# One norm chain per retention head, three output units taken together, and weight sums with fewer copies on the load queue

## The chip, the cores and the metric

The kernel runs on one core of a Trainium2 chip. A core has TensorE (PE in the profile: matmuls, with its weight loads in a row of their own, PEld), VectorE (DVE), ScalarE (ACT), GpSimd (POOL), a sync engine (SP) that only issues transfers, and 16 DMA engines shared by all queues. The metric is the time of one execution in device microseconds, the median of several runs. Each engine works through its own instructions in a fixed order, so an instruction that waits holds up all that stands behind it on that engine.

## What is computed

One decoder layer on 2048 tokens of 1024 channels: a mixer (retention heads beside a pooling mixer), a cross-attention into 256 memory tokens, and a gated MLP. The change lies in the mixer and in the preparation of weights:

```python
h = rmsnorm(x, mix_norm_g[l])
proj = h @ w_in[l]
q, k, v, g, u = jnp.split(proj, [R, 2 * R, 3 * R, 4 * R], axis=-1)
y_ret = jax.nn.silu(g) * head_rmsnorm(retention(q, k, v, positions), ret_gn_g[l])
y_pool = pool_mixer(u, pool_w[l], pool_scale[l])
x = x + jnp.concatenate([y_ret, y_pool], axis=-1) @ w_out[l]
x = x + cross_attn(rmsnorm(x, xa_norm_g[l]), mem_n, xa_wq[l], xa_wkv[l], xa_wo[l])
x = x + conv_glu_ffn(rmsnorm(x, ffn_norm_g[l]), ffn_w_up[l], ffn_conv_w[l], ffn_conv_b[l], ffn_w_down[l])
```

Retention has four heads of 128 channels and works in chunks of 128 tokens with a state carried from chunk to chunk. Each head's output is normalized per token (`head_rmsnorm`), gated by `silu(g)`, and goes with the four pooled groups into the output projection `w_out`.

## The kernel before, in words

**Blocks.** The 2048 tokens are two blocks of T = 1024, each of two halves of SUB = 512. A block goes through the mixer, the output projection and the attention; the MLP of both blocks follows at the end. Every product in full precision is three matmuls (high times high, high times low, low times high: `passes`, lines 265 to 269), so every tile that is a matmul operand is first split by ACT and DVE into a high and a low part (`split`, line 256, ACT at line 259, DVE in the helper at line 242).

**Order.** The text of the program gives priorities. A planner that simulates the engines then writes each engine's order from it, ahead of the run. `tc.issue_after(ins)` adds one rule: what is written inside the block is put behind `ins` on the engine of `ins`. Generators are stepped along the main loop: `behind[0]` holds the retention of a head, `under[0]` holds `weight_sums` (line 939).

**Mixer of the second block** (`head_projections`, line 1514). Eight "members" of two column groups each (`PAIRS`) are computed with seven items instead of eight; an item is 12 matmuls. The members are, in order, the pool groups 3 and 2 with a gate, the heads, and last the pool groups 0 and 1. When a member has given the second of q and k of a head, the head's `retention` (line 745) is stepped behind the seven items of the next member; the last head, 3, runs behind the last member. After each item two `step()` calls go on with the pooling windows (`pool_steps`), and in the last items `settle()` (line 1644) splits finished tiles into the places that the operand tables have left. The eight results are the tiles 0 to 3 (heads) and 4 to 7 (pool groups) of `mix`.

**Retention of a head** handles two halves a and c of four chunks. Each half has `scores` (PE line 766, transposes of k at 768), `states` (PE 777, then a chain of DVE steps through the four chunks), `values` (PE 790 and 792, then ACT squares at 796, the norm chain on DVE: scale, a reciprocal square root by three Newton steps (`rsqrt`, line 291), scale; then ACT scales at 804) and `mixed` (PE transposes at 809, a DVE step at 812). The steps of the two halves are offset, so that the chain of half a is done while half c is still at its scores. The PSUM tiles of these steps come from `aux()` (line 232), which goes in turn through three banks; the matmuls have five banks (`mmps`).

**Output projection** (`unit`, line 313, called at line 1872). A unit gives 128 output channels of the block: 8 tiles times 2 halves times 3 passes, 48 matmuls in two banks. Its weights are two loads on SP (lines 1869 and 1870) into one raw place, split into two pairs, and its tokens of x (`fetch_x`, line 546) come from two more loads. In the second block unit 0 takes the tiles in the order 7, 6, 0, 1, 2, 5, 3, 4 and all others in the order 0 to 7.

**Weight sums** (`weight_sums`, line 939). The seven-item products need sums of quarters of the weights. 42 jobs make them in DRAM: SP copies four quarters (lines 948 to 950, behind the load last noted in `fetched[0]`), then four accumulating DMAs on POOL's queue add up (lines 952, 953, 956, 959), each waiting for the one before. A job is five steps of the generator. The steps are taken along the main loop, in the attention `pace` of them per table (line 920), with `pace` 1 in the first block and 2 in the second.

Of the kernel before, what the change touches and what calls it, by code (L numbers as in the profile page):

```python
# [136 lines left out]
def trunk(ctx, tc, xT, memT, pos, w_qkgu, w_v, wkv, wqT, wo, wout_r, wout_p, poolT, w_up, w_dn, vecs, consts, outT):  # L137
# [19 lines left out]
    def new_s(dtype):  # L157
        return cp.tile([P, 2 * T], dtype, tag="S", name=nm("S"))

# [9 lines left out]
    S = new_s(F32)  # L169
    raws = Places([(R, j * T) for j in range(3)] + [(S, j * T) for j in range(2)], T)  # L170
# [73 lines left out]
    def ts(eng, out, a, s1, op0, s2=None, op1=None):  # L244
        if op1 is None:
            eng.tensor_scalar(out=out, in0=a, scalar1=s1, scalar2=None, op0=op0)
        else:
            eng.tensor_scalar(out=out, in0=a, scalar1=s1, scalar2=s2, op0=op0, op1=op1)
# [57 lines left out]
    turned = []  # L306
# [6 lines left out]
    def unit(raw, rhs, evac, order=range(KT)):  # L313


        hs = raw if isinstance(raw, list) else pairs(raw)
        ps = [mmps() for _ in range(NS)]
        for h in range(2):
            for s in range(NS):
                for j, k in enumerate(order[4 * h : 4 * h + 4]):  # L320
                    w = [hs[k // 4][:, i, k % 4 * P : (k % 4 + 1) * P] for i in range(2)]
                    passes(ps[s], w, rhs(k, s), h + j == 0, h == 1 and j == 3)
                next(behind[0], None)
                quarter[0] += 1
                if not slow[0] or quarter[0] % 2:
                    next(under[0], None)
                if h == 1:
                    evac(s, ps[s])
# [217 lines left out]
    def fetch_x(b, k):  # L546

        out = []
        for s in range(NS):
            out.append(TT.take())  # L550
            sp.dma_start(out[s].f[:, :SUB], xT[k * P : (k + 1) * P, b * T + s * SUB : b * T + (s + 1) * SUB])
        return out
# [192 lines left out]
    def retention(b, h, qkg, v, out):  # L745
# [4 lines left out]
        def col(ap, c):  # L750
            return ap[:, c * P : (c + 1) * P]
# [4 lines left out]
        class Half:  # L756
# [17 lines left out]
            def states(self):  # L774
                self.kv = aux()
                for c in range(4):
                    pe.matmul(col(self.kv, c), col(self.kn.f, c), self.ch(v, c, h * T), start=True, stop=True)  # L777
                self.cur = [None if b == 0 and self.s == 0 else st]
                for c in range(3):
                    nxt = col(self.kn.f, c)  # L780
                    if self.cur[c] is None:
                        dve.tensor_copy(nxt, col(self.kv, c))
                    else:
                        stt(nxt, self.cur[c], decay[h], col(self.kv, c))
                    self.cur.append(nxt)

            def values(self):
                y = aux()
                for c in range(4):
                    pe.matmul(col(y, c), col(self.pr.f, c), self.ch(v, c, h * T), start=True, stop=self.cur[c] is None)  # L790
                    if self.cur[c] is not None:
                        pe.matmul(col(y, c), self.ch(q, c), self.cur[c], start=False, stop=True)
                stt(st, self.cur[3], decay[h], col(self.kv, 3))
                ss, rr = small(), small()
                for c in range(4):
                    act.activation(col(self.pr.f, c), col(y, c), AF.Square, accum_out=ss[:, c : c + 1])
# [3 lines left out]
                if out is not None:  # L800
                    tt(dve, four(self.kn.f[:, :SUB]), four(y), bcast(rr, P), ALU.mult)
                else:
                    for c in range(4):
                        act.activation(col(self.kn.f, c), col(y, c), AF.Identity, scale=rr[:, c : c + 1])

            def mixed(self):
                mt = aux()
                for c in range(4):
                    pe.transpose(col(mt, c), col(self.kn.f, c), ident)
# [5 lines left out]
                for r in (self.pr, self.kn, gs[self.s]):  # L815
                    r.free()

        a, c = Half(0), Half(1)
        a.scores()
# [14 lines left out]
        if out is not None:  # L834
            q.free()
# [20 lines left out]
    def attention(sums, beside, pace):  # L856
# [39 lines left out]
        for i in range(2 * KT):  # L896
# [23 lines left out]
            for _ in range(pace):  # L920
                next(under[0], None)
# [17 lines left out]
    def weight_sums():  # L939
# [5 lines left out]
        for w, k0, n, to, in jobs:  # L945
            a11, a12, a21, a22 = (block(w, i // 2, i % 2, k0, n) for i in range(4))
            d = [to[i][:, : n * P] for i in range(4)]
            with tc.issue_after(fetched[0].ins):
                for i, a in ((2, a21), (0, a11), (1, a11), (3, a12)):
                    sp.dma_start(d[i], a)  # L950
# [8 lines left out]
            pool.dma_start(d[3], d[1], accum_op=ALU.add, max_dma_last_dim=2048)  # L959
# [554 lines left out]
    def head_projections(b, v, rb, tabs, t1, t2, z3, z4):  # L1514
# [4 lines left out]
        more = new_s(F32R)  # L1519
        raws = Places([(R, j * SUB) for j in range(5)], SUB)  # L1520
        side = Arena(R, 5 * SUB, 1, SUB).take().f
        prs = Places([(Q, j * T) for j in range(3)] + [(more, j * T) for j in range(2)], T)
# [175 lines left out]
        for at, (m, i) in enumerate(items):  # L1698
# [12 lines left out]
            step()  # L1711
            step()
            next(under[0], None)
            if m is members[-1]:
                if i in (1, 2, 4):
                    (t1, t2, t3)[(1, 2, 4).index(i)].free()
                if at >= len(items) - 6:
                    settle()
                    settle()
# [11 lines left out]
        spare = new_s(F32)  # L1731
        raws = Places([(R, j * T) for j in range(3)] + [(spare, j * T) for j in range(2)], T)
        prs = Places([(Q, j * T) for j in range(3)], T)
        return mix, spare
# [87 lines left out]
    for b in range(NB):  # L1822
# [19 lines left out]
        else:  # L1842
# [17 lines left out]
            mix, S = head_projections(b, v, rb, tabs, t1, t2, z3, z4)  # L1860
# [6 lines left out]
        for n in range(KT):  # L1867
# [4 lines left out]
            unit(raw, lambda k, s: [r[:, s * SUB : (s + 1) * SUB] for r in mix[k][1]], add_residual(b, n, xs, got=got), (0, 2, 3, 1, 4, 6, 7, 5) if b == 0 else (7, 6, 0, 1, 2, 5, 3, 4) if n == 0 else range(KT))  # L1872
# [24 lines left out]
        def opening(room, wv):  # L1897
# [3 lines left out]
            for kp in range(KT // 2):  # L1901
                wv.append(value_weights(kp))
# [63 lines left out]
    raws = Places([(R, j * SUB) for j in range(6)] + [(S, j * SUB) for j in range(4)], SUB)  # L1966
# [114 lines left out]
```

## Time and profile before

| | |
|---|---|
| median of 3 runs | 2480.15 us (2478.92 to 2484.32) |
| the profiled execution | 2478.89 us, its span 2477.0 us |
| PE busy | 2422.2 us, 98% of the span |
| DVE busy | 1730.7 us, 70% |
| ACT busy | 1283.2 us, 52% |
| POOL busy | 206.9 us, 8% |
| DMA moved | 501.56 MB, mean 202 GB/s |

The profile is of one execution. Its times are from the start of the span. A view by stretches gives, for each stretch of time, the busy time of each engine, the mean clock granted to TensorE (1.00 is full), the share of the 16 DMA engines that was busy (it can read a little over 1) and what they moved. A line of the view by time reads: start, duration, engine, line of the kernel, operation, output and inputs with their shapes, a count if several were merged, and in brackets the engine's idle time before it with what ended it. The wait view gives in total, times and longest. The stages of the part in question: first block's output projection from about 395 to 480 us, its attention to 575, the attention's output projection to 668, the second block's values to 714, its members to 904, its output projection to 1012, its attention to 1113.

### The profile page before, as it was taken

Reading aid. Unit: us, or ns where it says so; the run is one execution under the profiler, and the core shown is the slowest. Engines: PE = TensorE matmul, PEld = TensorE weight load, DVE = VectorE, ACT = ScalarE, POOL = GpSimd, SP = SyncE. Lnnn points to the kernel's source line nnn. Section 1 sums busy time; section 2 is a strip of 40 time slices with the busy share of each in tenths; the row PEclk is TensorE's granted clock in tenths of the full one; section 3 lists DMA queues with packets and bytes.
Section 4 is the critical chain, followed back from the end, with each engine's and each line's share of the span. In section 5 each row is a group of like instructions: output and inputs, shape, how many; then the busy total and the mean of one; then the engine's idle time right before and its main releaser. Section 6 shows DMA issues by size and latency. Waiting matters only on the chain.

```text
span 2477.0 us, 33287 instructions
## 1 busy us (share of the span) xinstructions
PE 2422.2 (98%) x11294; PEld 2018.0 (81%) x11294; DVE 1730.7 (70%) x2969; ACT 1283.2 (52%) x2303; POOL 206.9 (8%) x272
## 2 busy tenths in 40 slices
PE   6999999999999999999999999999999999999997
PEld 6888888878788877888888888888888888888886
DVE  8645576564676675575678876897667688867876
ACT  6333423443444443434655565665555677666663
POOL 1010111101001131200000010020000000000000
PEclk9999999999999999999999999999999999999998
DMA  8363789727748898966468665665546468768951
GB/s 315 95 167 115 222 209 244 226 51 223 219 125 199 203 258 246 250 204 249 145 198 278 210 190 158 218 222 169 161 154 216 136 223 302 246 189 280 344 171 69
DMA packets 274459, 501.56 MB, mean 202 GB/s; under 512 B 28784, under 2 KB 58096, under 8 KB 274288
## 3 DMA queue, kind: packets, MB, share of 16 engines
q1 hardware_dynamic: 225584, 428.11, 52.4%
q0 software_dynamic: 24192, 43.00, 10.8%
q10 hardware_dynamic: 24512, 28.32, 3.3%
q8 instruction: 89, 1.46, 0.2%
q14 instruction: 82, 0.67, 0.1%
HBM read 398.13 MB, written 187.17 MB: 236 GB/s over the span
## 4 chain that ended last, share of the span: by engine, by line
PE 88%; DMA 5%; DVE 4%; ACT 1%; issue 1%; SPq 0%; POOLq 0%; POOL 0%; ACTq 0%; DVEq 0%
PE mm L267 28%; PE mm L269 28%; PE mm L268 27%; DMA T<-xT 1%; DVE T L242 1%; DMA T<-Xd 1%; DVE Z L242 1%; PE aux L342 1%; PE aux L268 1%; PE aux L267 1%; PE aux L269 1%; PE aux L777 0%; DVE Q L242 0%; DMA T<-pos 0%; DMA Hd<-T 0%
## 5 line engine op out<-in xcount | busy, mean ns | idle before, releaser
L267 PE MATMUL mm<-G,Q 128*128 128x512 f32 (+1 forms) x1720 | 663.2, 386 | 23.5 <-ACT Q L259 14.6
L269 PE MATMUL mm<-G,Q 128*128 128x512 f32 (+1 forms) x1720 | 660.8, 385 | 6.3 <-DVE Q L242 6.1
L268 PE MATMUL mm<-G,Q 128*128 128x512 f32 (+1 forms) x1592 | 609.8, 383 | 0.2 <-DVE G L242 0.2
L268 PE MATMUL mm<-G,E 128*128 128x512 f32 x1084 | 421.6, 389 | 0.0
L267 PE MATMUL mm<-G,E 128*128 128x512 f32 x1084 | 420.2, 390 | 0.0
L269 PE MATMUL mm<-G,E 128*128 128x512 f32 x1084 | 419.2, 389 | 0.0
L267 PEld LDWEIGHTS mm<-G,Q 128*128 128x128 f32 x1720 | 326.6, 190 | 88.9 <-ACT Q L259 15.9
L269 PEld LDWEIGHTS mm<-G,Q 128*128 128x128 f32 x1720 | 326.4, 190 | 70.7 <-DVE Q L242 8.4
L268 PEld LDWEIGHTS mm<-G,Q 128*128 128x128 f32 x1592 | 302.1, 190 | 57.3 <-DVE G L242 1.5
L242 DVE TENSOR_TENSOR Z<-Z,mm 128x512 f32<-128x512 f32 x296 | 201.4, 681 | 101.2 <-PE mm L269 101.0
L251 DVE SCALAR_TENSOR_TENSOR Z<-Z,vecs 128x1024 f32<-128x1024 f32 x176 | 224.5, 1279 | 50.0 <-ACT Z L1104 46.4
L267 PEld LDWEIGHTS mm<-G,E 128*128 128x128 f32 x1084 | 203.5, 188 | 42.4 <-ACT Z L1186 0.3
L269 PEld LDWEIGHTS mm<-G,E 128*128 128x128 f32 x1084 | 203.5, 188 | 42.3
L268 PEld LDWEIGHTS mm<-G,E 128*128 128x128 f32 x1084 | 203.5, 188 | 42.1
L1041 ACT ACTIVATE E<-R 128x512 fp32r<-128x512 f32 (+1 forms) x165 | 101.5, 615 | 142.8 <-PE mm L268 135.3
L242 DVE TENSOR_TENSOR T<-T 128x512 f32<-128x512 f32 (+3 forms) x224 | 152.9, 688 | 23.2 <-ACT T L382 11.1
L242 DVE TENSOR_TENSOR Q<-R,Q 128x512 fp32r<-128x512 f32 x153 | 106.1, 696 | 74.5 <-ACT Q L259 50.8
L242 DVE TENSOR_TENSOR G<-T,G 128x512 fp32r<-128x512 f32 (+1 forms) x181 | 119.0, 673 | 42.5 <-ACT G L990 30.5
L1041 ACT ACTIVATE Q<-R 128x512 fp32r<-128x512 f32 (+1 forms) x157 | 96.9, 618 | 99.6 <-PE mm L268 73.8
L1104 ACT ACTIVATE Z<-Z,vecs 128x1024 f32<-128x1024 f32 x88 | 109.2, 1242 | 35.5 <-DVE Z L242 34.5
L990 ACT ACTIVATE G<-T 128x512 fp32r<-128x512 f32 x157 | 95.9, 625 | 54.5 <-DMA T<-Hd 27.3
L242 DVE TENSOR_TENSOR E<-R,E 128x512 fp32r<-128x512 f32 (+1 forms) x131 | 87.4, 671 | 51.2 <-ACT E L1041 42.3
(308 smaller groups left out, 3666.6 us busy)
## 6 DMA issues: line engine op xcount, KB each, us to landing
T<-Gd SPq DMA_DIRECT2D x168, 256.0 KB, 4.3
Gd<-Z SPq DMA_DIRECT2D x110, 256.0 KB, 2.7
R<-Ud SPq DMA_DIRECT2D x106, 256.0 KB, 2.7
Ud<-w_up SPq DMA_DIRECT2D x88, 256.0 KB, 6.1
R<-w_up SPq DMA_DIRECT2D x80, 256.0 KB, 3.0
S<-Ud SPq DMA_DIRECT2D x70, 256.0 KB, 2.8
T<-xT SPq DMA_DIRECT2D x64, 256.0 KB, 4.2
Gd<-T SPq DMA_DIRECT2D x56, 256.0 KB, 3.3
```

The costliest lines, as they stand in the source:

```text
L242: return eng.tensor_tensor(out=out, in0=a, in1=b, op=op)
L251: dve.scalar_tensor_tensor(out=out, in0=a, scalar=s, in1=b, op0=op0, op1=op1)
L267: pe.matmul(ps, lh, rh, start=start, stop=False, skip_group_check=more)
L268: pe.matmul(ps, lh, rl, start=False, stop=False, skip_group_check=more)
L269: latest[0] = pe.matmul(ps, ll, rh, start=False, stop=stop, skip_group_check=more)
L342: pe.matmul(ps[:, t : t + 1], ap, one, start=True, stop=more is None)
L990: act.activation(hi, x, AF.Copy)
L1041: act.activation(p2[:, 0, :w], self.raw[i].f[:, :w], AF.Copy)
L1104: act.activation(self.c[g].f, a[:, 2:], AF.Identity, bias=cb[:, f : f + 1], scale=cw[2][:, f : f + 1])
```

## The change

- `retention` in the second block (`out is None`): the two halves take each step right after one another, both halves' squares go into one tile of eight columns, and one norm chain serves both. `mixed` of both halves follows at the end. A head takes six steps rather than seven.
- In the last member, once the last head's chain has been written, the DVE part of `step()` and `settle()` is put behind that chain (`chained`).
- In the second block the first three output units run together: for each of the two halves of the tile order, all three units. The order is 6, 7, 0, 1, then 2, 4, 5, 3. Six PSUM banks hold the sums: five and the single one of `aux`. Their weights come in four loads per unit; the second pair of a unit is split when it is needed.
- The buffer S becomes two tiles: for the members one is a fourth operand pair (there were five) and the other holds two more raw places (seven for five).
- `weight_sums`: SP copies two quarters instead of four; the other two are copied by POOL's queue from the sum made before, and the remaining quarter is added there: six DMAs on POOL's queue instead of four. The generator still has five steps per job.
- `fetch_x` notes its load in `fetched[0]`, so sums stepped after it are put behind the loads of x. The value weights' loads are put behind the load noted last.
- In the first block's attention three steps of the sums per table instead of one; in the second still two.

```diff
     def units(weights, rhs, evacs, order, at):
+        ps = [[single() if NS * n + s == 5 else mmps() for s in range(NS)] for n, _ in enumerate(weights)]
+        for h in range(2):
+            for hs, evac, banks in zip(weights, evacs, ps):
+                if callable(hs[h]):
+                    hs[h] = hs[h]()
+                for s in range(NS):
+                    for j, k in enumerate(order[4 * h : 4 * h + 4]):
+                        w = [hs[at(k) // 4][:, i, at(k) % 4 * P : (at(k) % 4 + 1) * P] for i in range(2)]
+                        passes(banks[s], w, rhs(k, s), h + j == 0, h == 1 and j == 3)
...
         a, c = Half(0), Half(1)
+        if out is None:
+            both_ss, rr = small(8), small(8)
+            a.scores()
+            yield
+            c.scores()
+            a.states()
+            yield
+            c.states()
+            yield
+            a.values()
+            c.values()
+            v.free(h, 1)
+            k.free()
+            yield
+            ts(dve, both_ss, both_ss, xi2[:, h : h + 1], ALU.mult, EPS, ALU.add)
+            rsqrt(rr, both_ss)
+            chained.append(ts(dve, rr, rr, xi[:, h : h + 1], ALU.mult))
+            a.scaled(rr)
+            c.scaled(rr)
+            yield
+            a.mixed()
+            c.mixed()
+            return
...
-            for _ in range(pace):
+            for _ in range(4 - pace):
                 next(under[0], None)
...
-                for i, a in ((2, a21), (0, a11), (1, a11), (3, a12)):
+                for i, a in ((2, a21), (0, a11)):
                     sp.dma_start(d[i], a)
             yield
             pool.dma_start(d[2], a22, accum_op=ALU.add, max_dma_last_dim=2048)
             pool.dma_start(d[0], a21, accum_op=ALU.add, max_dma_last_dim=2048)
-            yield
-            yield
-            pool.dma_start(d[1], d[2], accum_op=ALU.add, max_dma_last_dim=2048)
-            yield
-            yield
-            pool.dma_start(d[3], d[1], accum_op=ALU.add, max_dma_last_dim=2048)
+            for at, was, a in ((1, 2, a11), (3, 1, a12)):
+                yield
+                pool.dma_start(d[at], d[was], max_dma_last_dim=2048)
+                yield
+                pool.dma_start(d[at], a, accum_op=ALU.add, max_dma_last_dim=2048)
...
-            step()
-            step()
+            with tc.issue_after(chained[-1].ins) if m is members[-1] and len(chained) == HEADS else nullcontext():
+                step()
+                step()
...
+            first, order = 3, (6, 7, 0, 1, 2, 4, 5, 3)
+            weights, evacs = [], []
+            for n in range(first):
+                raw = new_raw()
+                r = raw.rearrange("p (k c) -> p k c", c=P)
+                for at, w in ((0, WPd[n][:, 2:4]), (2, wout_r[n][:, 0:3]), (5, WPd[n][:, 0:2]), (7, wout_r[n][:, 3:4])):
+                    fetched[0] = sp.dma_start(r[:, at : at + w.shape[1]], w)
...
+            units(weights, mixed, evacs, order, order.index)
```

More of the change, by code (lines that the diff above doesn't have):

```diff
@@ L777, in states @@
                     pe.matmul(col(self.kv, c), col(self.kn.f, c), self.ch(v, c, h * T), start=True, stop=True)
[L778 removed]
+                self.cur = [a.after if out is None and self.s else None if b == 0 and self.s == 0 else st]
                 for c in range(3):
@@ L833, in retention @@
         v.free(h, 1)
-        if out is not None:
-            q.free()
+        q.free()
         k.free()
```

98 lines of the change are left out of this document (57 added, 41 removed).

## The prediction

> **What bounds the kernel now.** I read the page first, then the busy times by stretches, to find where TensorE is not at work, then the waits and the order in time at those places.
>
> ```profile
> span 2477.0 us, 33287 instructions
> PE 2422.2 (98%) x11294; PEld 2018.0 (81%) x11294; DVE 1730.7 (70%) x2969; ACT 1283.2 (52%) x2303; POOL 206.9 (8%) x272
> ```
>
> TensorE bounds: 98% of the span is matmul, and the change takes none away. All that can be won is time in which TensorE idles or runs at a lower clock. The MLP has none (first row below). The view by stretches shows, after the stretch's length, PE's busy time, then PEld, DVE, ACT, POOL, and last the granted clock, the DMA share and GB/s.
>
> ```profile
> 1260.00:2440.00 1180.00, 1179.67 (x5211) 976.72 (x5210) 911.04 (x1296) 736.04 (x1203) 53.74 (x82) 1.00 0.64 209
> 500.00:580.00 80.00, 78.04 (x370) 63.97 (x369) 51.86 (x120) 36.63 (x85) 0.66 (x1) 1.00 0.23 75
> 625.00:630.00 5.00, 1.04 (x3) 0.30 (x2) 2.18 (x4) 1.96 (x4) 0.81 (x1) 0.93 1.09 260
> 630.00:635.00 5.00, 4.58 (x11) 3.61 (x12) 4.08 (x7) 3.38 (x7) 1.63 (x2) 0.50 1.02 269
> 635.00:640.00 5.00, 5.00 (x21) 4.05 (x20) 4.48 (x8) 2.68 (x5) 0.00 (x0) 0.89 1.09 301
> 910.00:915.00 5.00, 4.50 (x28) 3.75 (x26) 0.00 (x0) 0.90 (x7) 0.00 (x0) 1.00 1.09 310
> 915.00:920.00 5.00, 3.97 (x25) 3.17 (x25) 4.72 (x16) 1.45 (x4) 4.17 (x5) 1.00 1.08 267
> 920.00:925.00 5.00, 1.86 (x8) 0.94 (x6) 4.39 (x22) 2.84 (x13) 2.44 (x4) 0.79 1.06 225
> 925.00:930.00 5.00, 4.69 (x12) 2.90 (x13) 4.96 (x15) 1.71 (x6) 3.64 (x6) 0.53 1.06 162
> 930.00:935.00 5.00, 3.46 (x11) 2.27 (x10) 3.61 (x6) 2.82 (x5) 1.76 (x3) 0.81 1.11 176
> 935.00:940.00 5.00, 5.00 (x20) 3.98 (x20) 1.30 (x3) 0.00 (x0) 0.83 (x2) 0.85 1.07 279
> ```
>
> Two holes. At 910 to 940, where the members end and the output projection begins, PE idles 0.50 + 1.03 + 3.14 + 0.31 + 1.54 = 6.5 us, and the clock below 1.00 costs 0.21, 0.47, 0.19 and 0.15 of four stretches of 5 us, 5.1 us: **11.6 us**. At 625 to 640 it idles 3.96 + 0.42 = 4.4 us and loses 0.07, 0.50 and 0.11 of 5 us, 3.4 us: **7.8 us**. Together 19.4 us, 0.8%: the most that these two places can give.
>
> **The hole at 910, part by part.** What PE waits for there:
>
> ```profile
> PE mm L267 <- ACT G L259: 3.0, 2, 1.5
> PE aux L809 <- ACT T L804: 1.6, 1, 1.6
> ```
>
> These are splits of late tiles into the operand table G, and the scaled halves of the last head. Both hang on the last norm chains, which I read from DVE's order in time (start, duration):
>
> ```profile
> 870.48 0.23 DVE L248 TENSOR_SCALAR sm<-sm,consts 128x4 f32<-128x4 f32 x1 [1.73 <-ACT T L796]
> 872.13 0.17 DVE L242 TENSOR_TENSOR sm<-sm 128x4 f32<-128x4 f32 x1
> ...
> 902.10 0.75 DVE L251 SCALAR_TENSOR_TENSOR Z<-aux,vecs,T 128x512 f32<-128x512 f32 x1 [1.08 <-PE aux L809]
> 903.97 0.68 DVE L242 TENSOR_TENSOR Z<-Z,mm 128x512 f32<-128x512 f32 x1
> 915.28 0.31 DVE L248 TENSOR_SCALAR sm<-sm,consts 128x4 f32<-128x4 f32 x1 [5.81 <-ACT T L796]
> 921.51 0.32 DVE L246 TENSOR_SCALAR sm<-sm,consts 128x4 f32<-128x4 f32 x1
> 921.98 0.23 DVE L248 TENSOR_SCALAR sm<-sm,consts 128x4 f32<-128x4 f32 x1 [0.15 <-ACT T L796]
> 927.76 0.22 DVE L246 TENSOR_SCALAR sm<-sm,consts 128x4 f32<-128x4 f32 x1
> 933.39 1.29 DVE L242 TENSOR_TENSOR E<-Z,E 128x512 fp32r<-128x512 f32 x2 [0.69 <-ACT E L259]
> ```
>
> A chain is 12 small DVE steps. Undisturbed, eight of them take 872.13 - 870.48 = 1.65 us, 0.21 us each, so 2.5 us a chain. The last head's two chains take 6.5 us (915.28 to 921.83) and 6.0 us (921.98 to 927.98), one after the other, since pooling steps stand between theirs. The last tile's split ends at 934.7. The last member was done at about 904 (its sum is taken up at 903.97), so for 30 us the output projection lives on tiles that are ready.
>
> *Cover.* How much work is ready? The pitch of a full-clock matmul is (884.59 - 882.09) / 11 = 0.227 us:
>
> ```profile
> 882.09 0.39 PE L267 MATMUL mm<-G,Q 128*128 128x512 f32 x1
> ...
> 884.59 0.39 PE L269 MATMUL mm<-G,Q 128*128 128x512 f32 x1
> ```
>
> Today five banks hold two and a half units: unit 0 can do tiles 7, 6, 0, 1, 2 (30 matmuls), unit 1 tiles 0, 1, 2 (18) and half of unit 2 nine: 57, or 12.9 us. After the change six banks hold three units, 72 matmuls on 6, 7, 0, 1 and 18 on tile 2: 90, or 20.4 us. **7.5 us more cover**. Beside it stands the last head's own work on PE; a step of a half is 1.06 us (the row of 887.78, quoted at the banks below), four such steps 4 us. PE would run dry at about 904 + 24 = 928.
>
> *When the last tile comes.* From 915 to 935 DVE is busy 4.72 + 4.39 + 4.96 + 3.61 = 17.7 us, of which the two chains are 24 steps, 5 us: 12.8 us of pooling, gating and splits stay, and they now stand behind the joint chain. So the last tile comes 12.8 us after that chain. The joint chain's end is not in the trace. Early bound: in the program it stands in the fifth of the last member's seven items, two items of 12 matmuls (5.4 us) before 904; it would end at 901. Late bound: it starts where half c's does today, 921.98, and ends at 924.5. I take the middle, 913: today the halves are offset, and half c's state step comes only when half a has given up its banks; side by side that wait goes. Then the last tile is there at 926, against a dry PE at 928. The bounds make it 914 (no stall) to 937 (9 us of stall). I keep 2 us for the order inside the second halves, where tile 4 comes early although it is pooled late. **Term: 11.6 - 2 = 9.6 us won**; bounds 11.6 won and 2.4 lost (9 us and today's 5.1 us of clock, against 11.6).
>
> The Trainium skill, "TensorE: Matmul & The Clock Gate", Part 1: The HAM clock gate, says that PE falls to half clock only after an idle window of about 3.4 us. Here 1.03 us idle at 915 kept the clock and 3.96 us at 625 was followed by 0.50. By it a stall of 2 us would cost no clock; if it did, by the ratio of today's hole, the term would be 8.0.
>
> **The hole at 625.** ACT stands behind a load of x, and PE behind ACT:
>
> ```profile
> 588.67 3.08 SPq L950 DMA_DIRECT2D Ud<-w_up  x5
> 596.14 7.31 SPq L950 DMA_DIRECT2D Ud<-w_up  x6
> 608.24 3.87 SPq L551 DMA_DIRECT2D T<-xT  x2
> ```
>
> ```profile
> 627.06 0.72 ACT L262 ACTIVATE G<-T,vecs 128x512 fp32r<-128x512 f32 x1 [13.99 <-DMA T<-xT]
> ```
>
> ```profile
> q1 hardware_dynamic: 225584, 428.11, 52.4%
> q0 software_dynamic: 24192, 43.00, 10.8%
> ```
>
> The load issued at 608.24 lands at 627, since sixteen copies of four jobs (eleven in these rows) were put in front; the DMA share is over 1. The change leaves SP eight. A copy is 0.262 MB; the SP queue took 0.524 x 2477 / 428.11 = 3.0 us per MB of all engines' time, so eight copies are 6.4 us, more than the 4 us that the stall lasts. But they are not gone: POOL's queue makes them two landings later, perhaps still ahead of x. Bounds 0 and 7.8; I take the middle: **4 us won**.
>
> The Trainium skill, "Trainium Kernel Development and Optimization", Key Constraints, says that DMAs of all queues share the same 16 engines and that another queue saves only issue time. The share of 1.09 agrees. By it alone this term would be 0 and the sum 2472.
>
> **Sums taken earlier.** Three steps per table instead of one are 32 steps, 6.4 jobs of five, brought into the first attention. A job is four SP-rate copies (4 x 0.262 x 3.0 = 3.2 us) and four adds at POOL's rate (0.108 x 2477 / 43.00 = 6.2 us per MB, 6.5 us): 9.7 us, so 62 us of DMA go to where the share is 0.23 over 80 us (18 us used). It fits, barely. What it may hold up is this load of x, behind which ACT has the exponentials:
>
> ```profile
> 529.66 0.63 ACT L378 ACTIVATE T<-T 128x512 f32<-128x512 f32 x1 [3.53 <-DMA T<-xT]
> 533.52 0.63 PE L884 MATMUL aux<-consts,T 128*128 128x128 f32 x4 [1.49 <-DVE T L246]
> ```
>
> Bounds 0 and 7.8 (the hole at 625); nearest is this row, at today's light load: I take **1 us lost**. That two more transfers of a job wait in turn costs nothing: the last sum's add is issued at 1053.91, the first sum of the MLP is read at 1188.32, and the 6.4 jobs come earlier.
>
> ```profile
> 1053.91 0.81 POOL L959 DMA_DIRECT2D Dd<-Dd  x1 [1.19 <-DMA Dd<-Dd]
> ```
>
> ```profile
> 1188.32 0.33 SPq L1035 DMA_DIRECT2D R<-Ud  x1
> ```
>
> **The rest.** Four operand pairs instead of five in the members: PE waits little for such pairs today (745 to 900 us; total, times, longest).
>
> ```profile
> PE mm L267 <- ACT S L1041: 1.0, 2, 0.5
> ```
>
> Bounds 1 won (no waits) and 3 lost (twice as much more); I take **0.5 lost**. Two more loads on SP for each of three units, and the first three joint chains (three times 2.5 us of DVE less): at nothing, since they lie under PE's matmuls with DVE at 70%. If that cover went, three units' six loads would cost some 0.3 us each of issue.
>
> **Sum:** 9.6 + 4 - 1 - 0.5 = 12.1 us. The profiled execution took 2478.89 us (span 2477.0 and 1.9 around it); it becomes 2466.8. The median shown is 1.3 us above it, so I forecast 2480.15 - 12.1 = **2468**.
>
> **Rivals.**
>
> *The late tiles stay late.* The chain ends at the late bound, since DVE holds its pooling back until the chain is done: 2.4 us lost there; with 4 won, 1 and 0.5 lost the time is 2480. For it: DVE idles 5.81 us ahead of 915.28 today and would do so again. Against: the chain is joint and undisturbed.
>
> *DMA only moves its crowd.* The hole at 625 stays and the attention gets one like it: 9.6 - 7.8 - 0.5 = 1.3 us won, 2479. For it: 62 us into 62 us of room. Against: the sums' transfers wait for one another, so they come spread out.
>
> *Slower: banks.* The aux tiles go in turn through three banks. Both halves' outputs now hold two of them from the squares until they are scaled, and the next head's first scores need the second one. Today the next head's scores ran inside head 2's chain:
>
> ```profile
> 887.78 1.06 PE L766 MATMUL aux<-E 128*128 128x128 f32 x8
> ```
>
> ```profile
> 895.96 1.14 ACT L804 ACTIVATE T<-aux,sm 128x128 f32<-128x128 f32 x4 [1.62 <-DVE sm L246]
> ```
>
> If they keep that place, PE waits from 887.8 until the scaling ends at 897.1, 9 us, at three heads' borders, 27 us: 2480.15 - 12.1 + 27 = 2495. It decides once a head lags its inputs by more than a member, 7 x 12 x 0.227 = 19 us: head 2 does today (its tile's DVE step at 902.10 is 14 us into the next head's time). Against: side by side a head no longer waits for its own first half, and the planner puts PE's steps behind their inputs; today PE waited for aux steps only as quoted.
>
> **How the numbers follow.** Forecast 0.62 (2459 to 2475); late tiles 0.15 (2480, between 2474 and 2484); DMA crowd 0.11 (2479); banks 0.12 (2485 to 2500). A measurement of this kernel can tell about 0.2%, 5 us, from no change: faster is below 2475.2, slower above 2485.1. Faster: 0.62 and a third of the two middle cases, 0.70. Within: the rest of those but 0.02, 0.16. Slower: 0.14. The range 2458 to 2483 leaves out the banks and the late tiles' worst, under 0.2.
>
> **What would show it.** Right: at 910 to 940 PE idles under 3 us with a granted clock of 1.00, one group of 128x8 small DVE steps per head, the last splits before 930; at 625 no idle stretch, fewer SP copies before the x load; DMA share over 0.6 at 500 to 580 and below 1 after 940. Wrong: idle at 920 to 935 on a split into E (late tiles), new waits of PE on aux tiles inside the members (banks), PE waiting on L884 or on x before 640 (DMA).

## The result and the profile after

The changed kernel takes 2484.99 us (median of 20 runs, 2475.43 to 2493.38), the kernel before, on the same chip, 2479.72 us (20 runs, 2475.12 to 2484.61). The ratio is 1.0016, with a 95% interval of 1.0006 to 1.0026: about 4 us slower by the ratio (the medians lie 5.3 us apart), where 12 us faster was forecast. By the ratio it is less than the 5 us that the prediction took as the least it could tell from no change. The forecast time of 2468.0 and its range up to 2483 are missed.

The page of the changed kernel, whose profiled execution took 2485.41 us. The last two rows are the DMA queues: packets, MB, share of 16 engines.

```profile
span 2483.6 us, 33188 instructions
PE 2421.9 (98%) x11294; PEld 2018.5 (81%) x11294; DVE 1728.7 (70%) x2921; ACT 1285.2 (52%) x2303; POOL 254.7 (10%) x356
...
q1 hardware_dynamic: 214352, 406.61, 49.0%
q0 software_dynamic: 30784, 64.50, 13.2%
```

PE has the same work to 0.3 us. DVE has 48 instructions fewer, POOL 84 more. So the 6.6 us of span are again idle time and clock. The view by stretches finds them (columns as in the prediction: length, PE, PEld, DVE, ACT, POOL, clock, DMA share, GB/s):

```profile
335.00:395.00 60.00, 60.00 (x299) 50.79 (x298) 46.63 (x116) 14.73 (x36) 0.00 (x0) 1.00 0.24 78
395.00:460.00 65.00, 65.00 (x288) 53.81 (x288) 34.22 (x53) 24.71 (x42) 18.49 (x26) 1.00 1.03 299
460.00:500.00 40.00, 31.65 (x136) 25.50 (x135) 19.86 (x48) 13.79 (x29) 14.92 (x20) 0.87 1.05 283
500.00:580.00 80.00, 75.91 (x357) 61.98 (x356) 47.43 (x111) 34.95 (x82) 37.24 (x51) 1.00 1.02 246
580.00:660.00 80.00, 79.65 (x356) 65.30 (x355) 36.12 (x58) 27.59 (x48) 13.21 (x18) 1.00 0.81 242
660.00:745.00 85.00, 81.47 (x363) 66.69 (x362) 63.90 (x124) 39.37 (x67) 2.19 (x3) 0.96 0.47 144
905.00:960.00 55.00, 52.69 (x267) 43.60 (x266) 32.55 (x74) 19.27 (x54) 11.79 (x16) 0.97 0.71 190
```

The same stretches of the kernel before, where they say something new:

```profile
335.00:395.00 60.00, 60.00 (x299) 50.78 (x299) 45.06 (x114) 13.54 (x36) 15.50 (x19) 1.00 0.95 225
395.00:460.00 65.00, 65.00 (x289) 53.83 (x288) 32.78 (x51) 23.27 (x40) 4.24 (x6) 1.00 0.69 209
460.00:500.00 40.00, 40.00 (x189) 33.30 (x188) 23.28 (x55) 18.10 (x37) 9.32 (x12) 1.00 1.03 283
```

I call the sum of idle time and lost clock of a stretch its loss; at 460 to 500 it is 8.35 + 0.13 x 40 = 13.6 us. In this table all profiles are read so (us). The clock is given to 0.01, so a stretch of 160 us is read to about 0.8 us. The last column is the time as a ratio to the kernel before on the same chip, with its interval; it differs by up to 0.0008 from the quotient of the medians. The kernel before took between 2479.72 and 2484.52 us (medians) on the chips used, so ratios are to be compared, not times.

| kernel | 460-500 | 500-580 | 580-660 | 660-745 | 745-905 | 905-960 | 960-1130 | ratio |
|---|---|---|---|---|---|---|---|---|
| before | 0 | 2.0 | 7.6 | 0 | 2.4 | 11.6 | 0.9 | 1 |
| after | 13.6 | 4.1 | 0.3 | 6.9 | 5.8 | 4.0 | 0.9 | 1.0016 [1.0006, 1.0026] |
| e1_pace_undone | 8.0 | 0 | 0 | 6.7 | 4.5 | 4.2 | 12.5 | 1.0013 [1.0002, 1.0023] |
| e2_pace_alone | 6.9 | 11.2 | 2.5 | 6.9 | 2.6 | 11.9 | 0.8 | 1.0063 [1.0051, 1.0076] |
| e3_compute_alone | 0 | 1.6 | 9.4 | 1.9 | 4.5 | 4.0 | 1.2 | 0.9965 [0.9952, 0.9978] |
| e4_pace_undone_five_pairs | 4.5 | 0 | 0.9 | 6.9 | 5.2 | 6.3 | 11.9 | 1.0032 [1.0020, 1.0044] |
| f1_copies_and_compute | 0 | 0 | 2.2 | 7.4 | 4.5 | 4.2 | 8.9 | 0.9985 [0.9972, 0.9998] |
| f2_order_and_compute | 11.7 | 0 | 9.5 | 3.4 | 5.1 | 4.2 | 12.5 | 1.0061 [1.0047, 1.0075] |
| f3_chain_without_units | 0 | 1.3 | 13.0 | 3.9 | 4.5 | 10.0 | 1.0 | 0.9992 [0.9982, 1.0002] |
| f4_compute_last_x | 0 | 0 | 0 | 10.9 | 4.5 | 6.9 | 1.4 | 0.9978 [0.9968, 0.9988] |
| g1_x_order_undone | 5.3 | 0 | 3.3 | 5.1 | 4.5 | 4.0 | 2.2 | 0.9957 [0.9940, 0.9974] |
| g2_copies_compute_pace2 | 2.2 | 0 | 2.0 | 6.1 | 4.5 | 3.0 | 4.0 | 0.9963 [0.9949, 0.9977] |
| g3_units_without_chain | 0 | 0.2 | 8.4 | 0.5 | 2.1 | 13.7 | 2.4 | 0.9989 [0.9978, 0.9999] |
| h1_first_block_note_undone | 2.1 | 0 | 1.2 | 7.9 | 4.5 | 4.3 | 0.6 | 0.9949 [0.9936, 0.9963] |

**Three things happened.** The hole at 910 went from 11.6 to 4.0 us (forecast: 2). The hole at 625 went too, but a hole of 6.9 us opened at 690. And a hole of 13.6 us opened at 460 to 500, where the prediction had seen none. There the changed kernel waits so (wait view of 455 to 505: total, times, longest; then rows by time):

```profile
PE aux L347 <- DVE T L242: 6.8, 1, 6.8
ACT Z L258 <- DMA R<-Md: 6.7, 1, 6.7
ACT T L387 <- DMA R<-Md: 6.5, 1, 6.5
DVE T L242 <- ACT T L387: 6.4, 1, 6.4
```

```profile
484.20 0.63 ACT L387 ACTIVATE T<-T 128x512 f32<-128x512 f32 x1 [6.51 <-DMA R<-Md]
484.87 0.69 DVE L242 TENSOR_TENSOR T<-T 128x512 f32<-128x512 f32 x1 [6.45 <-ACT T L387]
485.61 1.87 PE L347 MATMUL aux<-consts,T 128*128 128x1 f32 x8 [6.82 <-DVE T L242]
```

The end of the waiting is the same to 1.5 us on three engines. ACT idles 6.75 us ahead of one split of `Md`, the attention's matrix, and 6.51 us ahead of the squares of x (L387) that PE needs for the norm (L347). The profile puts both down to loads of `Md`, though the squares read none; the next in ACT's order that does is a split 0.5 us behind them. One of these loads, issued at 468.39, took 15.4 us to land, so it was there at 483.8, just when ACT goes on; why the squares stand still until then is not shown. The loads land late. The DMA view of 400 to 500 gives loads, KB of one and the median time to landing; before, then after:

```profile
R<-Md SPq DMA_DIRECT2D x5, 512.0 KB, 4.0
```

```profile
R<-Md SPq DMA_DIRECT2D x5, 512.0 KB, 12.4
```

And this is what fills the engines then, in SP's order of the kernel before and of the changed one:

```profile
336.70 2.58 SPq L950 DMA_DIRECT2D Ad<-w_qkgu  x4
...
381.98 3.00 SPq L950 DMA_DIRECT2D Ud<-w_up  x4
```

```profile
389.37 3.06 SPq L556 DMA_DIRECT2D T<-xT  x4
392.48 1.15 SPq L986 DMA_DIRECT2D Ad<-w_qkgu  x2
```

Before, five jobs of sums are started between 336.70 and 381.98, in the last part of the first block's mixer, when little else is loaded. After, the first of them starts at 392.48, behind the first loads of x, since these are now noted in `fetched[0]`. The rows of 335 to 395 show what that does: the DMA share falls from 0.95 to 0.24 and POOL has no work for 60 us; 0.71 x 60 = 43 us of DMA work are pushed into the time of the x loads and the `Md` loads, where the share goes from 0.69 to 1.03.

### The profile page after: what moved, and what is told of

The parts are those of the page before. It is cut to its first block, busy times and chain, and to the rows that moved or that the text cites. A ratio compares the mean times of both kernels' runs of the same rounds, so it can differ in the third digit from the quotient of the medians.

```text
span 2483.6 us, 33188 instructions
## 1 busy us (share of the span) xinstructions
PE 2421.9 (98%) x11294; PEld 2018.5 (81%) x11294; DVE 1728.7 (70%) x2921; ACT 1285.2 (52%) x2303; POOL 254.7 (10%) x356
## 3 DMA queue, kind: packets, MB, share of 16 engines
q0 software_dynamic: 30784, 64.50, 13.2%
## 4 chain that ended last, share of the span: by engine, by line
PE 86%; DMA 6%; DVE 4%; ACT 2%; issue 1%; SPq 0%; POOLq 0%; POOL 0%; DVEq 0%; ACTq 0%
PE mm L266 27%; PE mm L268 27%; PE mm L267 27%; DMA T<-xT 2%; DMA Ud<-w_up 1%; DVE T L242 1%; DMA T<-pos 1%; DMA T<-Xd 1%; DVE Z L242 1%; PE aux L266 1%; PE aux L771 1%; PE aux L782 1%; PE aux L267 1%; PE aux L798 1%; PE aux L268 1%
## 5 line engine op out<-in xcount | busy, mean ns | idle before, releaser
L266 PE MATMUL mm<-G,Q 128*128 128x512 f32 (+1 forms) x1745 | 672.4, 386 | 22.1 <-ACT Q L258 11.7
L268 PE MATMUL mm<-G,Q 128*128 128x512 f32 (+1 forms) x1745 | 669.1, 384 | 5.9 <-DVE Q L242 5.7
L267 PE MATMUL mm<-G,Q 128*128 128x512 f32 (+1 forms) x1617 | 619.5, 383 | 0.0
L266 PEld LDWEIGHTS mm<-G,Q 128*128 128x128 f32 x1745 | 331.0, 190 | 88.8 <-ACT Q L258 13.3
L268 PEld LDWEIGHTS mm<-G,Q 128*128 128x128 f32 x1745 | 330.3, 189 | 71.4 <-DVE Q L242 8.7
L267 PEld LDWEIGHTS mm<-G,Q 128*128 128x128 f32 x1617 | 306.8, 190 | 56.2
```

The source lines that it names most:

```text
L266: pe.matmul(ps, lh, rh, start=start, stop=False, skip_group_check=more)
L267: pe.matmul(ps, lh, rl, start=False, stop=False, skip_group_check=more)
L268: latest[0] = pe.matmul(ps, ll, rh, start=False, stop=stop, skip_group_check=more)
```

## The experiments

"The second block's part" or "compute" is the joint chain, the three units together and the two tiles S; "copies" are the two SP copies instead of four; "order" is the note of the x loads in `fetched[0]` with the value weights behind the load noted last; "pace" is three steps per table instead of one. The expectations name theories by letters: A, the pace makes the crowd at 400 to 500; B and later X, the order does; C, in the fourth run the four pairs make the members' idle time, and in the first and second of the second group the copies on POOL's queue make the crowd.

**e1_pace_undone**: the changed kernel, pace as before.

```diff
-            for _ in range(4 - pace):
+            for _ in range(pace):
```

> The changed kernel, but with one step of the sums per table in the first attention, as before, instead of three. Theory A (the 6.4 jobs brought into the first attention crowd the DMA engines, so the last loads of the memory table, issued at 466 to 469 us, land at 474 to 484, and ACT, DVE and PE wait in turn): the hole at 470 to 490 goes (8.4 us idle and 5 us of clock), the attention's other waits shrink, and the time falls by 13 to 17 us to about 2468 to 2472. Theory B (the sums' place behind the loads of x moves the output projection's own jobs there, and that is enough to fill the engines): DMA share stays over 1 from 400 to 500, the hole stays, and the time stays at 2482 or more.

Measured: 2486.82 us, ratio 1.0013. A holds for a part at most: without the extra steps 8.0 of the 13.6 us stay at 460 to 500, the share at 395 to 460 stays 1.03, and the time does not fall. The 4 us of loss at 500 to 580 go, but the sums that were taken there come late, and the second block's attention loses 12.5 us (PE waits for the scaled exponentials of DVE):

```profile
PE aux L920 <- DVE T L246: 9.1, 6, 2.9
```

**e2_pace_alone**: the kernel before with the new pace, the reverse of that diff.

> The kernel before with only the three steps per table in the first attention. Theory A: a hole of 8 to 14 us near 470 to 490, and a time 4 to 12 us above the kernel before, even though the sums after 900 us are fewer. Theory B: no hole there, since the output projection's jobs come early as before; the time is the same as before or some us less, because the sums at 900 to 960 are fewer.

Measured: 2499.64 us, ratio 1.0063, 16 us slower. The rows of 460 to 580:

```profile
460.00:500.00 40.00, 35.45 (x160) 29.38 (x159) 22.00 (x52) 16.71 (x36) 10.83 (x13) 0.94 0.97 263
500.00:580.00 80.00, 73.64 (x335) 60.30 (x334) 46.71 (x110) 31.00 (x78) 20.03 (x24) 0.94 0.85 205
```

Here A holds and B fails, though most of the loss comes at 500 to 580, and the time is 16 us above and not 4 to 12. So the pace does cost where each job has four SP copies; but by e1 undoing it in the changed kernel wins nothing.

**e3_compute_alone**: the changed kernel with pace, copies and order as before.

```diff
-            fetched[0] = sp.dma_start(out[s].f[:, :SUB], xT[...])
+            sp.dma_start(out[s].f[:, :SUB], xT[...])
...
-                with tc.issue_after(fetched[0].ins):
-                    wv.append(value_weights(kp))
+                wv.append(value_weights(kp))
```

> Only the second block's part of the change: joint norm chain, three units together, late tiles last, four operand pairs and seven raw places. The sums have four copies on the load queue, one step per table, and no order behind the loads of x, as before. Both theories: the first attention is as before, without the hole at 470 to 490; the hole at 910 to 940 (11.6 us) falls to about 4, while the hole at 625 (7.8 us) stays; the members lose about 3 us. Time 2473 to 2477. If the members' loss is larger, or the late tiles still stall, 2479 or more.

Measured: 2475.02 us, ratio 0.9965, 8.7 us faster. The second block's part does what was forecast of it; all of the loss is in the transfers.

**e4_pace_undone_five_pairs**: e1 with five operand pairs and five raw places in the members.

```diff
-        more = new_s(F32R, 0)
+        more = [new_s(F32R, j) for j in range(2)]
```

> As the run with the attention's steps undone, and with five operand pairs and five raw places in the members, as before, instead of four and seven. Theory C (the fourth-pair limit makes PE wait on ACT's conversions in the members: 5.8 us idle there instead of 2.4): idle of PE from 745 to 905 falls back to about 2.5 us and the time is 3 to 4 us below that run. Theory D (it is the two halves taken together, with their squares and scales in one burst on ACT, that delays the conversions): no difference over 1 us.

Measured: 2492.07 us, ratio 1.0032. The members' loss is 5.2 us, against 4.5 in e1: the four pairs are not its cause. The time is 0.0019 above e1's, which was not followed up.

**f1_copies_and_compute**: e3 with the new sums, so compute and copies.

```diff
-                for i, a in ((2, a21), (0, a11), (1, a11), (3, a12)):
+                for i, a in ((2, a21), (0, a11)):
```

> The second block's part of the change, plus only the sums with two SP copies instead of four; steps of the attention, the place of the sums behind the x loads and the value weights' place are as before. Theory X (the place of the sums behind the x loads makes the crowd at 400 to 500): no crowd here, DMA share at 420 to 460 below 0.8, no idle of PE at 460 to 500, and the eight copies fewer close the hole at 580 to 660, of which most comes back at 660 to 745: 2470 to 2475. Theory C (copies on POOL's queue make the crowd): share at 420 to 460 above 0.9, loss at 460 to 500 of 4 us or more: 2479 to 2485.

Measured: 2478.63 us, ratio 0.9985, above X's 2470 to 2475 and below C's range. There is no loss at 460 to 500, as X says, and the share at 420 to 460 is 0.77, below X's 0.8. What was missed is the end: in the table 960 to 1130 loses 8.9 us. The sums wait longer for one another and come into the second block's attention, as in e1.

**f2_order_and_compute**: e3 with the notes, so compute and order.

> The second block's part of the change, plus only the notes of the x loads, so that the sums stand behind the x loads and the value weights behind the load noted last; four SP copies per job and the attention's steps as before. Theory X: DMA share at 420 to 460 above 0.9, Md loads land in 10 us or more, loss at 460 to 500 of 4 us or more, nothing won at 625, since the sixteen copies there stand behind a load of VWd and not behind one of x: 2480 to 2490. Theory C: as the second block's part alone, 2473 to 2477.

Measured: 2497.66 us, ratio 1.0061: 0.0096 above e3, 24 us, for the notes and the place of the value weights that goes with them. X holds in its place (11.7 us at 460 to 500) and underrates the size; the rest comes late, 12.5 us at 960 to 1130. At 580 to 660 nothing is won, since the sixteen copies there stand behind a load of `VWd`.

```profile
395.00:460.00 65.00, 63.32 (x278) 51.83 (x277) 28.44 (x45) 20.83 (x36) 17.32 (x21) 1.00 1.06 291
460.00:500.00 40.00, 31.94 (x132) 25.50 (x131) 23.93 (x54) 17.21 (x34) 9.89 (x12) 0.91 1.08 304
```

**f3_chain_without_units**: e3, its output projection unit by unit in the old order.

```diff
-        if b:
+        if False:
             first, order = 3, (6, 7, 0, 1, 2, 4, 5, 3)
```

> The second block's part of the change without the three output units run together: one norm chain per head, steps and settles behind the last chain, four pairs; the output projection unit by unit in its old order. If the longer cover of ready matmuls closes the hole at 910 to 940 (prediction: 7.5 us more), that hole is back at 6 us or more of idle and clock, 2478 to 2483. If the joint chain, which brings the last tile sooner, closes it, the loss there stays near 4 us and the time is that of the second block's part alone, 2473 to 2477.

Measured: 2480.87 us, ratio 0.9992. The hole is back: 10.0 us at 905 to 960, against 11.6 before and 4.0 in e3. The joint chain by itself does not close it.

**g3_units_without_chain**: the reverse, the kernel before with only the three units together (`units`, four weight loads, the new order).

> The kernel before with nothing changed but the first three output units of the second block run together (weights in four loads, the order 6, 7, 0, 1, 2, 4, 5, 3); two norm chains per head, five pairs, sums as before. If the cover of ready matmuls alone closes the hole at 910 to 940: 4 us or less of loss there, the members keep their 2.4 us of idle, 2470 to 2475. If the joint chain is needed too (without it the last tiles come later than the cover lasts): 6 us or more there, 2475 to 2480.

Measured: 2478.71 us, ratio 0.9989. The hole does not shrink, it gets larger, 13.7 us, by one wait in the midst of ready matmuls:

```profile
PE aux L815 <- ACT T L810: 8.7, 1, 8.7
```

```profile
920.00:925.00 5.00, 0.52 (x5) 0.28 (x3) 4.69 (x14) 1.97 (x10) 3.27 (x4) 0.81 1.12 290
925.00:930.00 5.00, 0.76 (x3) 0.54 (x3) 3.55 (x13) 1.58 (x5) 2.73 (x4) 0.50 1.12 223
```

PE's order has the transposes of the last head (L815) ahead of output matmuls, and they wait for the scaling (L810) behind a norm chain that shares DVE with the pooling. PE goes through its list in order, so ready work behind a waiting transpose covers nothing. Neither half of the change does it; together they do.

**f4_compute_last_x**: e3 with the sums of the second block's values behind the last load of x.

```diff
         under = paused
+        if b + 1 < NB:
+            fetched[0] = last_x[0]
```

> The second block's part of the change, and the sums of the second block's values stage put behind its last load of x (sixteen SP copies move from 585 to 605 to behind 657); all other parts of the DMA order as before. Theory G (the x loads alone bound the stage to the norm, so what is won at 625 is given back at 680): the hole at 580 to 660 goes (9.4 to under 1 us), 660 to 745 loses 5 to 8 us: 2470 to 2474. Theory H (the sixteen copies are the whole hole): both stages under 3 us, 2464 to 2469. If the crowd only moves, the members' idle at 745 to 905 rises above 6 us and the time stays 2474 to 2478.

Measured: 2478.06 us, ratio 0.9978, no better than e3. The rows:

```profile
580.00:660.00 80.00, 80.00 (x362) 66.53 (x361) 48.05 (x73) 35.38 (x59) 3.89 (x5) 1.00 0.55 170
660.00:745.00 85.00, 75.76 (x331) 61.23 (x331) 53.84 (x108) 32.61 (x54) 12.57 (x16) 0.98 0.78 203
```

The hole at 625 goes completely, and 10.9 us stand at 660 to 745 instead. G holds for the exchange, not for the time: what is won is given back in full, and more than G's 5 to 8 us, since the copies now run beside the loads of that later stretch (share 0.78 against 0.53 in e3). At 905 to 960 it loses 6.9 us instead of 4.0, which was not followed up. The members' loss did not rise.

**g1_x_order_undone**: the changed kernel but for the notes of the x loads (the first line of e3's diff).

> The whole change but for the notes of the x loads: joint chain, three units, two SP copies per job, three steps per table of the first attention stay. Theory X (the place of the sums behind the x loads makes the hole at 460 to 500): the share at 420 to 460 falls below 0.9, that hole (13.6 us in the changed kernel) falls below 4, the late crowd of the run with copies and compute at 960 to 1130 (8.9 us) is gone too since the sums are done early: 2470 to 2475, the best so far. Theory P (three steps per table are by themselves too much for the first attention, as they were with four SP copies): 8 us or more of loss at 460 to 580, 2479 to 2487.

Measured: 2472.44 us, ratio 0.9957. Against 1.0016 with them, the notes cost 0.0059, 15 us. The share at 420 to 460 is 0.84, below X's 0.9, the loss at 460 to 500 5.3 us (a little over the 4 of X), that of 960 to 1130 2.2. P fails: with two SP copies a job and the old place, three steps per table are no harm.

**g2_copies_compute_pace2**: f1 with two steps per table in the first attention.

> As the run with copies and compute, but two steps of the sums per table in the first attention, between the one of before and the three of the changed kernel; sums not behind the x loads. Theory X: no hole at 460 to 580 yet, the crowd at 960 to 1130 smaller than its 8.9 us, 2471 to 2476. Theory P: 3 to 6 us of loss at 460 to 580, 2476 to 2481.

Measured: 2474.04 us, ratio 0.9963. As X has it: 2.2 us at 460 to 500, nothing at 500 to 580, and 4.0 instead of 8.9 at 960 to 1130. From one step over two to three (f1, g2, g1) the ratio is 0.9985, 0.9963, 0.9957: sums taken early are a gain here. Two and three are not told apart, and g1 has the value weights behind the load noted last besides.

**h1_first_block_note_undone**: the changed kernel, the x loads noted in the second block only.

```diff
-            fetched[0] = sp.dma_start(out[s].f[:, :SUB], xT[...])
+            one = sp.dma_start(out[s].f[:, :SUB], xT[...])
+            if b:
+                fetched[0] = one
```

> The whole change, but the loads of x in the first block's output projection are not noted, so the sums before them keep their old place ahead of these loads; the notes of the second block's loads stay. Theory X, one place: the loss comes only from the five jobs pushed behind the first block's x loads and onto the attention's first loads: share at 420 to 460 below 0.9, loss at 460 to 500 below 6 us, time as with all notes undone, 2470 to 2475. Rival: the notes of the second block cost as well, by sums that come late (hole at 960 to 1130 above 6 us): 2477 to 2483.

Measured: 2471.89 us, ratio 0.9949 [0.9936, 0.9963], the lowest ratio of all, though its interval overlaps those of g1 and g2. One note in one place turns the change from 4 us slower to 12.6 us faster. The rows:

```profile
335.00:395.00 60.00, 60.00 (x300) 50.75 (x299) 46.79 (x116) 14.75 (x36) 15.17 (x20) 1.00 0.81 190
395.00:460.00 65.00, 65.00 (x289) 53.81 (x288) 33.89 (x53) 24.88 (x43) 10.18 (x14) 1.00 0.87 236
460.00:500.00 40.00, 37.86 (x179) 31.25 (x178) 25.01 (x62) 16.98 (x37) 7.54 (x11) 1.00 0.97 298
500.00:580.00 80.00, 80.00 (x380) 65.97 (x379) 48.59 (x109) 33.58 (x79) 38.81 (x52) 1.00 1.07 255
```

The sums are back at 335 to 395 (share 0.81, POOL 15.17 us), only 2.1 us are lost at 460 to 500, and at 500 to 580 a share of 1.07 does PE no harm: it waits for nothing there. The notes of the second block cost nothing that shows (0.6 us at 960 to 1130, and the time is that of g1): the rival falls.

## Why the prediction was wrong, step by step

**The missed step: the order of the sums.** The prediction counted the SP copies ahead of the x load at 608 (it said eight are left; the changed kernel has six there) and gave the diff's new note in `fetch_x` no term at all: it stood at nothing, without a reason. Of a step that is moved, every DMA and every queue counts: in the first block's output projection the note moves five jobs past the loads of x, onto the attention's first loads. The runs with and without it (after against g1 and h1, by the ratios) put 15 to 17 us on it. That is about the whole difference between forecast and result, 16 us by the ratio, and more than all that was to be won.

**"Sums taken earlier", 1 us lost.** "It fits, barely" was right of the room at 500 to 580 and wrong of its price as long as the note stands (after loses 4.1 us there, e1 none) or a job has four SP copies (e2 loses 11.2). With two copies and without the note more steps are a gain (g2, g1 against f1), since the sums otherwise meet the second attention; the prediction had the bounds of this term at 0 and 7.8 lost and thought of no gain. The rival "DMA only moves its crowd" came nearest: it had a crowd of sums beside an attention load, at 7.8 us. But it had it from the extra steps and beside a load of x, with the hole at 625 staying; it came from the note, beside the loads of `Md`, with 13.6 us, and the hole at 625 went.

**The hole at 625, 4 us won.** It went (7.6 to 0.3 us), and came back 65 us later (0 to 6.9). The waits of 660 to 745 in the changed kernel:

```profile
691.60 0.79 PE L371 MATMUL aux<-Q,ones 128*128 128x512 f32 x1 [2.80 <-DVE Q L242]
692.19 0.63 PE L267 MATMUL mm<-G 128*128 128x512 f32 x1
...
695.60 0.63 PE L268 MATMUL mm<-G 128*128 128x512 f32 x1
696.03 0.48 PE L266 MATMUL mm<-G 128*128 128x512 f32 x1
```

PE waits there for the norm over all of the second block's x, and DVE's order shows what holds that norm up:

```profile
680.15 0.16 DVE L247 TENSOR_SCALAR sm<-aux 128x8 f32<-128x8 f32 x1
...
686.03 0.69 DVE L242 TENSOR_TENSOR T<-T 128x512 f32<-128x512 f32 x1 [4.50 <-ACT T L1532]
...
690.36 0.17 DVE L1775 COPY rn<-sm 128x8 f32<-128x8 f32 x1
```

```profile
685.27 0.72 ACT L1532 ACTIVATE T<-T,vecs 128x512 f32<-128x512 f32 x1 [5.92 <-DMA T<-xT]
```

The sums over x are there at 680.15. The norm's small steps then take until 690.5: among them in DVE's order stand steps of `quarter_sums` (line 1518), the preparation of the members' operands, and the first of these waits 4.50 us for ACT, as ACT waits for loads of x that SP issues only from 679.66 on. The kernel before has the same order, but DVE waits 1.80 us at that place; in the other runs it is 3.2 to 5.1, but for f4, where the first norm is done before it. In every profile of this table 580 to 745 loses between 6.7 and 16.9 us in sum, whether sixteen copies stand ahead of the x loads, six or eight do, or none. So behind the hole at 625 a second wait of nearly the same cost seems to stand. That this foreign step makes it is read from the traces; no run moves it. The rule quoted from the Trainium skill, "Trainium Kernel Development and Optimization", Key Constraints, by which this term was 0, came nearer in the number than my 4, but not for its reason: the hole at 625 did go.

**The hole at 910, 9.6 us won.** 11.6 became 4.0, 7.6 won; the table's other runs with both halves have 3.0 to 4.3, but f4 (6.9) and e4 (6.3). The size was nearly right, the way to it only in part. The chain of the last head and the last split, in e3:

```profile
916.91 0.23 DVE L247 TENSOR_SCALAR sm<-sm,consts 128x8 f32<-128x8 f32 x1 [3.73 <-ACT T L804]
...
919.20 0.28 DVE L246 TENSOR_SCALAR sm<-sm,consts 128x8 f32<-128x8 f32 x1
...
936.26 0.69 DVE L242 TENSOR_TENSOR E<-Z,E 128x512 fp32r<-128x512 f32 x1 [0.70 <-ACT E L258]
```

The joint chain runs undisturbed in 2.6 us, as forecast (2.5). It ends at 919.5, not 913, and the last split at 937, 17.5 us behind it and not 12.8; the kernel before had that split at 934.7. So the tiles do not come sooner: 937 is the prediction's late bound, at which it put 9 us of stall, and DVE does idle ahead of the chain (3.73 us), as its rival of the late tiles said. That the loss is 4 us even so is in part luck: the tile came later than forecast, and PE had more to do until then than was counted. What closes the hole is that PE has enough to do (f3: 10.0 without the units) and meets no late transpose on the way (g3: 13.7 without the chain). The residue is 4 us and not 2.

**Four pairs, 0.5 lost.** The members lose 4.5 to 5.8 us in all runs that have the joint chain and 2.1 to 2.6 in those that have not (before, e2, g3). Five pairs do not help (e4), nor does leaving the units out (f3). So 2 to 3 us go with the chain and its steps, not with the pairs; which of them was not tried. (The bound of 3 lost was itself off: twice as much again of 1.0 us is 2.)

**Banks.** No such wait appears: in the wait view of the changed kernel at 745 to 905 PE waits for ACT's operands alone. This rival was the one on the slower side, and the kernel is slower for another reason.

**The sum by the best run.** h1, which has all but the one note, is 12.6 us faster (9.2 to 15.9), and the forecast was 12.1. That the numbers meet is partly luck: 7.3 of it is the hole at 910, and at 580 to 745 it loses 1.5 us more than before; its profile is 6.1 us shorter than the profile of before, and the rest lies between profile and medians. In 0 to 395, which the table leaves out, PE idles 19.9 to 21.1 us in the kernels with two tiles S and 22.2 to 23.2 in the three with one (before, e2, g3); why was not tried.

## What to carry to other kernels

A rule "put behind the load noted last" is an order for every user of that note: where a diff adds a note, go through all the places that read it, above all those that were early and filled idle transfer time, and look at what they will now run into. A hole that is closed can come back at the next wait behind it, here a norm chain with a foreign step among its own; look for that next wait before counting the gain. Cover counts only up to the first instruction in PE's order that waits, so more ready work and earlier late work have to come together.

## What the runs showed of the hardware

**Half clock after a short stop, but not after every one.** In g1 PE idles 1.70 us ahead of the norm's matmuls (a group of eight with one column each), and the clock falls all the same:

```profile
480.11 1.67 PE L347 MATMUL aux<-consts,T 128*128 128x1 f32 x8 [1.70 <-DVE T L242]
481.63 0.77 PE L268 MATMUL mm<-G 128*128 128x512 f32 x1
482.20 0.63 PE L266 MATMUL mm<-G 128*128 128x512 f32 x1
```

From 482.20 the pitch is 0.43 us instead of 0.227, for 5 us, and the stretch of 460 to 500 loses 3.6 us of clock on 1.7 of idle time. In the changed kernel 2.80 us ahead of 691.60 are followed by the same pitch until 696. In h1 PE idles longer at the place of g1's stop, and the clock stays at 1.00:

```profile
481.38 1.05 PE L347 MATMUL aux<-consts,T 128*128 128x1 f32 x8 [2.14 <-DVE T L242]
```

In g2 it is the same with 2.22 us. The prediction took from the Trainium skill, "TensorE: Matmul & The Clock Gate", Part 1: The HAM clock gate, that PE falls to half clock only after an idle window of about 3.4 us; the stops of 1.70 and 2.80 us differ from that, read as the length of one stop. By these rows the length of one stop does not decide; what does is not shown.

**A copy on POOL's queue costs the engines about what it costs on SP's.** q0 took 0.108 x 2477 = 267.5 us of all engines' time for 43.00 MB before and 0.132 x 2483.6 = 327.8 us for 64.50 MB after: 60 us for 21.5 MB of plain copies, 2.8 us per MB if the adds cost the same in both, beside 3.0 on SP's queue over all its transfers. The 6.2 us per MB that the prediction read from q0 are the price of the accumulating transfers alone.

**Spread.** The changed kernel's 20 runs lie within 18 us, those of the kernel before within 9.5.
